# A two-layer trunk on one Trainium2 core: three of the four pairs of output tiles of the FFN's down projection by Strassen's product

## The chip, the core and the metric

The kernel runs on one core of one Trainium2 chip. The metric is the device time in microseconds (us) of one execution, as the median of several runs. TensorE multiplies (PE, its weight loads PEld), VectorE is DVE, ScalarE ACT, GpSimd POOL; SyncE (SP) issues most DMAs.

## The reference

Two layers on x of 512 rows (S) by 1024 columns (D), all in float32; D_FF is 2816.

```python
def conv_ffn(h, up, dw, dw_b, down):
    u = causal_dwconv(h @ up, dw, dw_b)
    gate, val = split_cols(u, [D_FF, D_FF])
    return (jax.nn.silu(gate) * val) @ down
...
# each layer: x = x + mixers(rmsnorm(x)) @ out;  x = x + conv_ffn(rmsnorm(x), ...);  at the end rmsnorm(x)
```

The four mixers (two kinds of attention, RWKV-7, a convolution module) are not touched by the change.

## The kernel before, in words

Everything is held transposed: channels lie on the 128 partitions, the 512 rows of the sequence along the free axis. So x is 8 tiles of 128 x 512 (`x[0..7]`, named x604 to x611 in layer 0's second half), and the FFN's inner activations are 22 tiles.

A float32 product is made of three float16 products. A weight tile is loaded from DRAM in float32 into a staging tile `st` (SP, L196) of 128 x 1024 (8 blocks of 128 x 128) or less, then split into a high part (ScalarE, L211) and a low part (VectorE, L212) in a tile `hl`. Activations are split in the same way. `mm3` (L231 to L236) gives three matmuls for each block of weights, hi x hi, hi x lo and lo x hi; each is 512 columns (the sequence) or 256 wide and loads its own weights.

`weights` (L1118 to L1141) lists all weight tiles of the program in the order of use. `next_w` pops a split tile and keeps `depth` further ones split ahead; `_split` and `w_load` are where the staging tiles come from: two of `wst`, five split tiles of `whl`, and for part of the FFN's tiles a further ring of FST = 2 staging and FHL = 4 split tiles in the FFN's own pool `fp`. Loads and splits are put ahead of other work by a high priority; the order on each engine's queue is fixed when the program is built. An engine works through its queue in that order, and a load waits until its buffer is free.

The up projection is `ffn_up` (L1092 to L1116): 44 tiles of 8 blocks, 24 matmuls each. For each pair (gate, value) the PSUM tile g goes through the three-tap convolution (L1103 ScalarE, L1104 and L1105 VectorE) into u, then tanh, two multiplications (L1109, L1111) and the split into one `act` tile of 2 x 512 (L1113 ScalarE, L1114 VectorE).

The down projection is `project` (L1065 to L1090). For each of 8 output tiles it takes three weight tiles (8, 8 and 6 blocks) and makes 22 x 3 matmuls into one PSUM bank; the last output tile is made in two halves of 256 columns, so that the norm behind it can begin on the first half. `back` (L1027 to L1029) adds a finished product to the residual x on VectorE; `norm_add` (L379 to L390) squares it on ScalarE and adds the squares on GpSimd; `norm_rb` sums over partitions by a matmul on TensorE, and `norm_apply` writes the next layer's input, or `finish` the output. `out_second` (L1044) is the mixers' output projection ahead of the up projection, with the same additions on GpSimd.

```python
        for m in range(NK - tail):
            hls = [self.next_w() for _ in range(nw)]
            ps = self.gbank()
            tile_(ps, hls, full)
            self.back(m, ps, full, scale)
            self.norm_add(m, full, norm_eng)
```

## Time and profile before

| | |
|---|---|
| median of 3 runs | 1348.14 us (1345.51 to 1348.59) |
| profiled execution | 1351.01 us, span 1349.2 us, mean granted clock 0.989 |
| TensorE busy | 1301.4 us (96% of the span) |
| VectorE, ScalarE, GpSimd busy | 903.1, 609.9, 117.7 us |
| DMA | 119.96 MB, 89 GB/s on the mean |

The profile is of one execution on the chip. Busy times are by engine and may overlap; the clock is TensorE's granted share of full speed. In the rows further below a line such as L212 is a line of the kernel; `hl<-st,hl` says what a group of instructions writes and reads.

### The profile page before, as it was taken

To read this page: it belongs to the slowest core of one execution; us is meant where nothing else is said; L and a number is where in the kernel's file an instruction comes from. 1 tells how busy PE (TensorE), PEld (TensorE's weight loads), DVE (VectorE), ACT (ScalarE), POOL (GpSimd) and SP (SyncE) were. 2 spreads that over 40 slices of the span, in tenths; PEclk is the share of its full clock that TensorE was granted. 3 is DMA by queue.
4 is the path that set the end of the run, shared out by engine and by line. 5 is a ranking of instruction groups with operands and counts; after the bars stand their busy time and mean duration, and the time that the engine had idled before them with its cause. 6 is when DMAs were issued, how large, how long until landed. Compare 5 with 4: busy or idle time off the path is not lost.

```text
span 1349.2 us, 22863 instructions
## 1 busy us (share of the span) xinstructions
PE 1301.4 (96%) x9198; PEld 738.1 (55%) x9198; DVE 903.1 (67%) x1770; ACT 609.9 (45%) x1115; POOL 117.7 (9%) x180
## 2 busy tenths in 40 slices
...
GB/s 221 157 85 60 118 33 10 1 71 110 78 94 110 94 109 95 141 167 121 52 101 107 80 78 103 10 3 32 94 51 109 107 96 108 96 103 188 70 28 63
DMA packets 41864, 119.96 MB, mean 89 GB/s; under 512 B 4896, under 2 KB 11680, under 8 KB 41760
## 3 DMA queue, kind: packets, MB, share of 16 engines
...
## 4 chain that ended last, share of the span: by engine, by line
PE 81%; DVE 12%; ACT 2%; DMA 2%; issue 2%; SPq 0%; DVEq 0%; ACTq 0%
PE g L234 21%; PE g L235 21%; PE g L236 21%; DVE cacc L755 4%; PE v L922 3%; PE t L911 2%; DVE hl L212 2%; PE s L891 2%; PE r L578 1%; PE r L234 1%; PE r L235 1%; PE r L236 1%; DVE e L894 1%; DMA st<-in_wi_dram 1%; ACT e L898 1%
## 5 line engine op out<-in xcount | busy, mean ns | idle before, releaser
L236 PE MATMUL g<-hx,hl 128*128 128x512 f16 (+1 forms) x1008 | 368.6, 367 | 0.0
L234 PE MATMUL g<-hx,hl 128*128 128x512 f16 (+1 forms) x1008 | 367.8, 367 | 0.8 <-DVE q L787 0.8
L235 PE MATMUL g<-hx,hl 128*128 128x512 f16 (+1 forms) x1008 | 368.2, 367 | 0.3 <-DVE hx L423 0.3
L212 DVE SCALAR_TENSOR_TENSOR hl<-st,hl 128x1024 f16<-128x1024 f32 (+2 forms) x200 | 238.6, 1195 | 115.8 <-ACT hl L211 114.2
L211 ACT ACTIVATE hl<-st 128x1024 f16<-128x1024 f32 (+2 forms) x200 | 204.4, 1026 | 213.4 <-PE g L236 149.3
L234 PEld LDWEIGHTS <-hl 128*128 128x128 f16 x1724 | 170.1, 99 | 159.5 <-issue 5.2
L236 PEld LDWEIGHTS <-hl 128*128 128x128 f16 x1724 | 169.3, 98 | 157.0 <-issue 2.2
L235 PEld LDWEIGHTS <-hl 128*128 128x128 f16 x1724 | 169.6, 98 | 154.2 <-issue 2.5
L235 PE MATMUL g<-act,hl 128*128 128x512 f16 (+1 forms) x396 | 140.7, 355 | 0.0
L236 PE MATMUL g<-act,hl 128*128 128x512 f16 (+1 forms) x396 | 140.7, 355 | 0.0
L234 PE MATMUL g<-act,hl 128*128 128x512 f16 (+1 forms) x396 | 140.7, 355 | 0.0
L1104 DVE SCALAR_TENSOR_TENSOR u<-g,d_fdw,u 128x511 f32<-128x511 f32 x82 | 61.5, 750 | 95.7 <-ACT u L1103 95.7
L1103 ACT ACTIVATE u<-g,par,d_fdw 128x512 f32<-128x512 f32 x82 | 63.7, 777 | 101.6 <-PE g L236 101.4
L755 DVE SCALAR_TENSOR_TENSOR cacc<-gl,d_cdw,cacc 128x511 f32<-128x511 f32 (+14 forms) x120 | 90.0, 750 | 1.3
L1028 DVE SCALAR_TENSOR_TENSOR x<-g,x 128x512 f32<-128x512 f32 (+1 forms) x62 | 34.9, 568 | 83.3 <-PE g L236 83.1
L909 POOL TENSOR_SCALAR e<-e,den 128x512 f32<-128x512 f32 (+3 forms) x96 | 55.9, 595 | 316.4 <-DVE den L901 207.4
L390 POOL TENSOR_TENSOR acc<-acc,sq 128x256 f32<-128x256 f32 (+1 forms) x38 | 41.7, 1098 | 462.4 <-ACT sq L383 405.5
L894 DVE CUSTOM_DVE_ANT_0 e<-s,con 128x512 f32<-128x512 f32 (+3 forms) x96 | 46.8, 488 | 34.2 <-PE s L891 24.4
L1113 ACT CAST act<-u 128x512 f16<-128x512 f32 x44 | 27.1, 617 | 93.2 <-DVE u L1111 93.2
L1105 DVE SCALAR_TENSOR_TENSOR u<-g,d_fdw,u 128x510 f32<-128x510 f32 x82 | 61.4, 748 | 2.8
L898 ACT ACTIVATE e<-e,mx 128x512 f32<-128x512 f32 (+3 forms) x96 | 53.1, 556 | 17.0 <-DVE mx L896 16.9
L383 ACT ACTIVATE sq<-x 128x256 f32<-128x256 f32 (+1 forms) x54 | 24.5, 467 | 74.9 <-DVE x L1028 71.1
...
## 6 DMA issues: line engine op xcount, KB each, us to landing
st<-in_up_dram SPq DMA_DIRECT2D x88, 512.0 KB, 3.5
st<-in_wi_dram SPq DMA_DIRECT2D x40, 512.0 KB, 3.4
st<-in_dn_dram SPq DMA_DIRECT2D x32, 512.0 KB, 3.7
st<-in_wo_dram SPq DMA_DIRECT2D x16, 512.0 KB, 3.5
st<-in_dn_dram SPq DMA_DIRECT2D x16, 384.0 KB, 3.2
...
```

The costliest lines, as they stand in the source:

```text
L211: act = nc.scalar.activation(hl[:, 0, :cols], st[:, :cols], AF.Copy, scale=SW)
L212: dve = nc.vector.scalar_tensor_tensor(hl[:, 1, :cols], st[:, :cols], SW, hl[:, 0, :cols], op0=ALU.mult, op1=ALU.subtract)
L234: nc.tensor.matmul(ps, hl[:, 0, w], hx[:, 0, cols], start=start, stop=False)
L235: nc.tensor.matmul(ps, hl[:, 0, w], hx[:, 1, cols], start=False, stop=False)
L236: nc.tensor.matmul(ps, hl[:, 1, w], hx[:, 0, cols], start=False, stop=stop)
L755: nc.vector.scalar_tensor_tensor(acc[:, s:512], gl[:, 0:512 - s], wj, acc[:, s:512], op0=ALU.mult, op1=ALU.add)
L894: nc.vector.tensor_tensor_reduce(es[i], ps[:, o:o + w], mask[:, 384 - 128 * t:512], op0=ALU.add, op1=ALU.max, scale=1.0, scalar=-3e38, acc ...
L898: nc.scalar.activation(es[i], es[i], AF.Exp, scale=SC, bias=mx[:, i:i + 1], accum_out=den[:, i:i + 1])
L909: nc.gpsimd.tensor_scalar(es[i], es[i], den[:, i:i + 1], 1.0, op0=ALU.mult, op1=ALU.mult)
L1103: act = nc.scalar.activation(u, ps, AF.Identity, scale=w[:, 88 + ch:89 + ch], bias=self.p("fb", ch))
L1104: stt(u[:, 1:512], ps[:, 0:511], w[:, 44 + ch:45 + ch], u[:, 1:512], op0=ALU.mult, op1=ALU.add)
L1105: dve = stt(u[:, 2:512], ps[:, 0:510], w[:, ch:ch + 1], u[:, 2:512], op0=ALU.mult, op1=ALU.add)
```

## The change

The residual product is y = W^T a, with 8 output tiles and 22 tiles to sum over. The change takes the output tiles in pairs, the channel tiles of the activations in pairs, and the sequence in two halves of 256: each is a 2 x 2 product of blocks, A the weights (A11 to A22), Q the activations (Q11 to Q22). For three of the four pairs of output tiles, `project_fast` makes seven products of blocks (Winograd's form of Strassen's) in place of eight:

- P1 = A11 Q11, P2 = A12 Q21, P4 = A22 T4 use weights as they are; P5 = S1 T1, P6 = S2 T2, P7 = S3 T3 and P3 = S4 Q22 use sums of weights: S1 = A21 + A22, S3 = A11 - A21, S2 = S1 - A11, S4 = A12 - S2. T1 to T4 are differences of activations.
- Each product is 11 blocks x 3 matmuls of 256 columns. `back` adds the finished PSUM tile to the one or two places of x that it belongs to, some after more products have been added to it in PSUM.
- `act_pair` makes T1 to T4 on VectorE, with four subtractions of 256 columns for each pair of channel tiles, and splits two times 1024 columns (Q's, then T's) instead of two times 512.
- `make_sums` loads the four quarters of a pair of output tiles again, in float32, and makes S1 to S4 in place. The first pair is cut into three parts of 4, 4 and 3 blocks; parts 0 and 1 are summed on GpSimd during the up projection, in tiles `dq` that share the buffers of hx; part 2 and the other pairs (two parts of 6 and 5 blocks) on VectorE, in a pool `dp` of ten tiles `dw`, which is opened when the up projection's pool `up` has been closed and takes its place. S tiles are then split as staged weights are.
- The fourth pair is made as before (66 matmuls of 512 columns for tile 6, two halves for tile 7).
- The further ring of staging and split tiles is gone; some split tiles lie in `act` or `dw` buffers.

```diff
-FST, FHL = 2, 4
+DW = 10
...
-        if ring:
-            st = self.fp.tile([128, 1024], F32, tag="fst", bufs=FST, name=self.n("st"))
+
+
+    def w_load(self, src, cols, home=None):
+        if home == "act":
+            st = self.fp.tile([128, 1024], F32, tag="act", bufs=NF // 2, name=self.n("st"))
         else:
             st = self.wst.tile([128, 1024], F32, tag="st", name=self.n("st"))
-        nc.sync.dma_start(st[:, :cols], src)
+        self.nc.sync.dma_start(st[:, :cols], src)
         return st
+
+    def w_pair(self, home):
+        if home == "act":
+            return self.fp.tile([128, 2, 1024], F16, tag="act", bufs=NF // 2, name=self.n("hl"))
+        if home == "dw":
+            return self.dp.tile([128, 2, 768], F16, tag="dw", bufs=DW, name=self.n("hl"))
+        return self.whl.tile([128, 2, 1024], F16, tag="hl", name=self.n("hl"))
...
+        st = src() if callable(src) else self.w_load(src, cols, home)
+        hl = self.w_pair(home)
...
-            self.spare = self.ffn
             return self.stash.pop(0)
         hl = self.next_w()
-
-        ps = self.rbank() if self.spare else self.gbank()
-        self.spare = False
+        ps = self.gbank()
+        for k in range(NK):
+            self.mm3(ps, hl, k, hx[k], slice(0, 512), k == 0, k == NK - 1)
+        return ps
+
+    def gemm_up(self, hx, m):
+
+        if self.stash:
+            if self.todo and len(self.ready) <= self.depth:
+                self.prefetch()
+            return self.stash.pop(0)
+        hl = self.next_w()
+        ps = self.rbank() if m == HEAD else self.gbank()
...
-    def project(self, rhs, order, tail, scale, norm_eng):
-        nc = self.nc
-        nk = len(order)
...
+    Q12, Q11, Q22, Q21, T3, T1, T2, T4 = range(8)
+
+    def act_pair(self, fp, q):
+
+        nc = self.nc
+        a = fp.tile([128, 2, 8 * 256], F16, tag="act", bufs=NF // 2, name=self.n("act"))
+        src = q.rearrange("p a b -> p (a b)")
+
+        def split(cols):
+            nc.scalar.copy(a[:, 0, cols], src)
+            nc.vector.tensor_tensor(a[:, 1, cols], src, a[:, 0, cols], op=ALU.subtract)
+
+        def sub(o, i, j):
+            nc.vector.tensor_tensor(q[:, o % 4], q[:, i % 4], q[:, j % 4], op=ALU.subtract)
+
+        split(slice(0, 1024))
+        sub(self.T1, self.Q12, self.Q11)
+        sub(self.T3, self.Q22, self.Q12)
+        sub(self.T2, self.Q22, self.T1)
+        sub(self.T4, self.Q21, self.T2)
+        split(slice(1024, 2048))
+        return a
+
+
+    FAST = {"P1": ("A11", Q11), "P2": ("A12", Q21), "P3": ("S4", Q22), "P4": ("A22", T4), "P5": ("S1", T1),
+            "P6": ("S2", T2), "P7": ("S3", T3)}
+    RAW = {"A11": (0, 0), "A12": (0, 1), "A21": (1, 0), "A22": (1, 1)}
+
+
+    PARTS = (((0, 4), (4, 8), (8, 11)),) + (((0, 6), (6, 11)),) * 3
+
+    def fast_order(self, mp):
+        n = range(len(self.PARTS[mp]))
+        if mp:
+            return [(p, h) for p in ("P1", "P5", "P6", "P3", "P7", "P2", "P4") for h in n]
+        raw = ("P1", "P2", "P4")
+        return ([(p, h) for p in raw for h in n[:-1]] + [(p, n[-1]) for p in raw] +
+                [(p, h) for p in ("P5", "P6", "P3", "P7") for h in n])
...
+    def down_items(self, l):
+        items = []
+        for mp in range(NK // 2 - 1):
+            for p, h in self.fast_order(mp):
+                w = self.FAST[p][0]
+                src, n = self.quarter(l, mp, w if w in self.RAW else "A11", h)
+                if w not in self.RAW:
+                    src = lambda w=w, key=(mp, h): self.sums[key][w]
+                items.append((src, n))
+        for w in ("A11", "A12", "A21", "A22"):
+            for h in range(2):
+                items.append(self.quarter(l, NK // 2 - 1, w, h) + (("dw",) if w[1] == "2" else ()))
+        return items
+    def make_sums(self, l, mp, h):
+        nc = self.nc
+        b = {}
+        for name in ("A22", "A11", "A21", "A12"):
+            src, n = self.quarter(l, mp, name, h)
+            if mp == 0 and h < 2:
+                t = self.hxp.tile([128, 512], F32, tag="hx", bufs=NK, name=self.n("dq"))
+            else:
+                t = self.dp.tile([128, 768], F32, tag="dw", bufs=DW, name=self.n("dw"))
+            b[name] = t[:, :n]
+            nc.sync.dma_start(b[name], src)
+        tt = (nc.gpsimd if mp == 0 and h < 2 else nc.vector).tensor_tensor
+        tt(b["A22"], b["A21"], b["A22"], op=ALU.add)
+        tt(b["A21"], b["A11"], b["A21"], op=ALU.subtract)
+        tt(b["A11"], b["A22"], b["A11"], op=ALU.subtract)
+        tt(b["A12"], b["A12"], b["A11"], op=ALU.subtract)
+        self.sums[mp, h] = {"S1": b["A22"], "S2": b["A11"], "S3": b["A21"], "S4": b["A12"]}
+    def project_fast(self, l, acts, scale, norm_eng):
+        c1, c2 = self.HALVES[1], self.HALVES[0]
+        full = slice(0, 512)
+        self.make_sums(l, 0, 2)
+        self.after = ()
+        ahead = {0: {9: 0, 15: 1}, 1: {5: 0, 9: 1}, 2: {}}
+        for mp in range(NK // 2 - 1):
+            m = 2 * mp
+            parts, order = self.PARTS[mp], self.fast_order(mp)
+            x = {"11": (m, c1), "12": (m, c2), "21": (m + 1, c1), "22": (m + 1, c2)}
+            A, B, C = self.gbank()[:, 0:256], self.rbank()[:, 0:256], self.rbank()[:, 0:256]
+            reg = {"P1": A, "P2": B, "P3": C, "P4": A if mp else self.rbank()[:, 0:256], "P5": C, "P6": A, "P7": A}
+            adds = {"P1": ("11",), "P2": ("11",), "P5": ("22",), "P6": ("12",), "P3": ("12",),
+                    "P7": ("22",) if mp else ("22", "21"), "P4": ("21",)}
+            seen = set()
+            for step, (p, h) in enumerate(order):
+                if step in ahead[mp]:
+                    self.make_sums(l, mp + 1, ahead[mp][step])
+                r = reg[p]
+                q = 256 * self.FAST[p][1]
+                k0, k1 = parts[h]
+                hl = self.next_w()
+                for k in range(k0, k1):
+                    self.mm3(r, hl, k - k0, acts[k], slice(q, q + 256), k == k0 and id(r) not in seen,
+                             k == k1 - 1, True)
+                seen.add(id(r))
+                if h < len(parts) - 1:
+                    continue
+                for o in adds[p]:
+                    self.back(x[o][0], r, x[o][1], scale)
+            for i in range(2):
+                self.norm_add(m + i, full, norm_eng)
...
+        m = NK - 2
+        ps = self.gbank()
+        tile_(ps, [self.next_w() for _ in range(4)], full)
+        self.back(m, ps, full, scale)
+        self.norm_add(m, full, norm_eng)
         self.depth = HEAD
-        hls = [[self.next_w() for _ in range(nw)] for _ in range(tail)]
+        m += 1
+        hls = [self.next_w() for _ in range(4)]
         for cols in self.HALVES:
-            for i in range(tail):
-                m = NK - tail + i
-                ps = self.gbank()[:, 0:256]
-                tile_(ps, hls[i], cols)
-                self.back(m, ps, cols, scale)
-                self.norm_add(m, cols, nc.vector if m < NK - 1 else None)
+            ps = self.gbank()[:, 0:256]
+            tile_(ps, hls, cols)
+            self.back(m, ps, cols, scale)
+            self.norm_add(m, cols)
             yield cols
...
+            if i in (NF - 8, NF - 5):
+                self.make_sums(l, 0, int(i == NF - 5))
+            if i == NF - 2:
+                self.depth = 4
...
-            nc.vector.tensor_tensor(us[0], us[0], us[1], op=ALU.mult)
-            a = fp.tile([128, 2, 512], F16, tag="act", bufs=NF, name=self.n("act"))
-            nc.scalar.copy(a[:, 0], us[0])
-            nc.vector.tensor_tensor(a[:, 1], us[0], a[:, 0], op=ALU.subtract)
-            acts.append(a)
+            if i % 2 == 0:
+                q = up.tile([128, 4, 256], F32, tag="q", bufs=1, name=self.n("q"))
+            nc.vector.tensor_tensor(q[:, 2 * (i % 2):2 * (i % 2) + 2].rearrange("p a b -> p (a b)"), us[0], us[1],
+                                    op=ALU.mult)
+            if i % 2:
+                acts.append(self.act_pair(fp, q))
...
-                items.append((a["up"][l, m], 1024, m < HEAD or m % 2 == 1))
-            for m in range(NK):
-                for g in range(3):
-                    k1 = min(8, NF - 8 * g) * 128
-                    items.append((a["dn"][l, m, :, 1024 * g:1024 * g + k1], k1, m == NK - 1 or (3 * m + g) % 2 == 1))
+                items.append((a["up"][l, m], 1024, "act" if m < HEAD else None))
+            items += self.down_items(l)
...
+                with pool(f"up{l}") as up:
+                    hf = self.new_hx(up, "hf")
+                    for cols in self.out_second(OTAIL):
+                        self.norm_apply(self.d["gf"], hf, cols)
+                    self.gemm_head(hf, HEAD)
+                    self.depth = 2
+                    acts = self.ffn_up(l, fp, up, hf)
...
-                for cols in self.project(acts, range(NF), 1, 1.0 / (SW * SA), nc.gpsimd):
+                with pool(f"dp{l}") as self.dp:
+                    for cols in self.project_fast(l, acts, 1.0 / (SW * SA), nc.gpsimd):
```

The list of weights in DRAM is laid out for this by quarters. In the order rows that follow, hl is a split weight tile, st a staged one, dq and dw quarters of weights or their sums, q a pair's Q's or T's, act its split tile, x the residual, g and r PSUM banks.

VectorE of the changed kernel, layer 0, from the last splits of activations (L1089) to the first sum (L1152) of the down projection:

```order
L215 SCALAR_TENSOR_TENSOR hl997_5948<-st996_5946,hl997_5948 128x384
L1092 TENSOR_TENSOR q944_5734<-q944_5734 128x256
L215 SCALAR_TENSOR_TENSOR hl998_5963<-dq863_5167,hl998_5963 128x512
L1092 TENSOR_TENSOR q944_5734<-q944_5734 128x256
L215 SCALAR_TENSOR_TENSOR hl999_5978<-dq897_5406,hl999_5978 128x512
L1039 SCALAR_TENSOR_TENSOR x604_3375<-g984_5874,x604_3375 128x256
L1092 TENSOR_TENSOR q944_5734<-q944_5734 128x256
L1039 SCALAR_TENSOR_TENSOR x604_3375<-r985_5875,x604_3375 128x256
L1089 TENSOR_TENSOR act954_5808<-q944_5734,act954_5808 128x1024
L1039 SCALAR_TENSOR_TENSOR x605_3376<-r987_5877,x605_3376 128x256
L1152 TENSOR_TENSOR dw980_5862<-dw982_5866,dw980_5862 128x384
```

All of these are new: the last split of the T's stands behind the split of the last raw weights of the first pair and two splits of sums, and the first sum on VectorE behind it.

SP of the changed kernel at the same place, the loads of the first pair's last raw parts, of the second pair's first raw tiles, and of the quarters for the sums (L1150):

```order
L196 DMA st992_5912<-in_dn_dram 128x384
L196 DMA st994_5929<-in_dn_dram 128x384
L196 DMA st996_5946<-in_dn_dram 128x384
L196 DMA st1018_6157<-in_dn_dram 128x768
L196 DMA st1020_6172<-in_dn_dram 128x640
L1150 DMA dw980_5862<-in_dn_dram 128x384
L1150 DMA dw981_5864<-in_dn_dram 128x384
L1150 DMA dw982_5866<-in_dn_dram 128x384
L1150 DMA dw983_5868<-in_dn_dram 128x384
L1150 DMA dw1002_6017<-in_dn_dram 128x768
```

Before, this queue held staged weights alone; now the quarters stand in it, and dw981 lies where tiles of the up projection were.

VectorE at the end of layer 0's down projection, before:

```order
L1028 SCALAR_TENSOR_TENSOR x609_3380<-g1013_6220,x609_3380 128x512
L212 SCALAR_TENSOR_TENSOR hl1024_6379<-st1023_6377,hl1024_6379 128x768
L212 SCALAR_TENSOR_TENSOR hl1032_6399<-st1031_6397,hl1032_6399 128x1024
L1028 SCALAR_TENSOR_TENSOR x610_3381<-g1021_6306,x610_3381 128x512
L1028 SCALAR_TENSOR_TENSOR x611_3382<-g1033_6402,x611_3382 128x256
```

and of the changed kernel:

```order
L215 SCALAR_TENSOR_TENSOR hl1091_6865<-st1090_6863,hl1091_6865 128x768
L215 SCALAR_TENSOR_TENSOR hl1093_6870<-st1092_6868,hl1093_6870 128x640
L215 SCALAR_TENSOR_TENSOR hl1096_6945<-st1095_6943,hl1096_6945 128x1024
L215 SCALAR_TENSOR_TENSOR hl1098_6950<-st1097_6948,hl1098_6950 128x1024
L1039 SCALAR_TENSOR_TENSOR x610_3381<-g1085_6852,x610_3381 128x512
L215 SCALAR_TENSOR_TENSOR hl1100_6955<-st1099_6953,hl1100_6955 128x1024
L215 SCALAR_TENSOR_TENSOR hl1102_6960<-st1101_6958,hl1102_6960 128x1024
L1039 SCALAR_TENSOR_TENSOR x611_3382<-g1103_6963,x611_3382 128x256
```

The update of x610 (output tile 6) now has four splits right ahead of it, the last two of the next layer's first weights (hl1096, hl1098).

## Rows read from the trace of the kernel before

**Rows 1.** The page: busy us (share of span) and instructions by engine; chain by engine.
```profile
PE 1301.4 (96%) x9198; PEld 738.1 (55%) x9198; DVE 903.1 (67%) x1770; ACT 609.9 (45%) x1115; POOL 117.7 (9%) x180
...
PE 81%; DVE 12%; ACT 2%; DMA 2%; issue 2%; SPq 0%; DVEq 0%; ACTq 0%
```
**Rows 2.** Windows of layer 0's up and down projection: PE, PEld, DVE, ACT, POOL, clock, DMA, GB/s.
```profile
331.00:560.00 229.00, 228.98 (x1166) 113.72 (x1164) 164.81 (x234) 106.16 (x146) 1.07 (x2) 1.00 0.30 94
560.00:675.00 115.00, 115.00 (x601) 58.62 (x600) 38.86 (x48) 30.77 (x36) 10.71 (x7) 1.00 0.39 124
```
**Rows 3.** Timeline of PE (start, us, instruction), first and last of each stretch.
```profile
554.80 0.38 PE L236 MATMUL g<-hx,hl 128*128 128x512 f16 x1
...
560.41 0.38 PE L235 MATMUL g<-hx,hl 128*128 128x512 f16 x1
...
663.83 0.27 PE L234 MATMUL g<-act,hl 128*128 128x256 f16 x1
...
667.65 0.27 PE L236 MATMUL g<-act,hl 128*128 128x256 f16 x1
```
**Rows 4.** Groups of PEld by form: xcount | busy us, mean ns | idle before, releaser.
```profile
L235 PEld LDWEIGHTS <-hl 128*128 128x128 f16 x1724 | 169.6, 98 | 154.2 <-issue 2.5
```
**Rows 5.** Groups of DVE by form, the same columns.
```profile
L212 DVE SCALAR_TENSOR_TENSOR hl<-st,hl 128x1024 f16<-128x1024 f32 x176 | 215.8, 1227 | 88.9 <-ACT hl L211 87.3 <-PE g L236 1.2
...
L1114 DVE TENSOR_TENSOR act<-u,act 128x512 f16<-128x512 f32 x44 | 30.4, 691 | 26.0 <-ACT act L1113 26.0
...
L423 DVE TENSOR_TENSOR hx<-nt,hx 128x256 f16<-128x256 f32 x64 | 26.1, 426 | 0.5
...
L212 DVE SCALAR_TENSOR_TENSOR hl<-st,hl 128x768 f16<-128x768 f32 x16 | 15.3, 955 | 26.8 <-ACT hl L211 26.8
...
L1028 DVE SCALAR_TENSOR_TENSOR x<-g,x 128x256 f32<-128x256 f32 x28 | 11.6, 420 | 26.8 <-PE g L236 26.6
```
**Rows 6.** Groups of ACT by form: the splits of 1024 and 768 columns.
```profile
L211 ACT ACTIVATE hl<-st 128x1024 f16<-128x1024 f32 x176 | 184.5, 1050 | 155.9 <-PE g L236 98.8 <-DMA st<-in_wi_dram 19.9 <-DMA st<-in_dn_dram 14.6
...
L211 ACT ACTIVATE hl<-st 128x768 f16<-128x768 f32 x16 | 13.4, 840 | 37.3 <-PE g L236 32.5 <-issue 4.6 <-DMA st<-in_dn_dram 0.2
```
**Rows 7.** Groups of POOL by form: the norm's additions of 512 columns.
```profile
L390 POOL TENSOR_TENSOR acc<-acc,sq 128x512 f32<-128x512 f32 x14 | 21.7, 1547 | 441.9 <-ACT sq L383 385.2 <-issue 56.6
```
**Rows 8.** Timeline of SP: start, us that one issue takes, load.
```profile
606.17 0.33 SPq L196 DMA_DIRECT2D st<-in_wi_dram  x1
```
**Rows 9.** DMA issues of the whole span: xcount, KB each, median us to landing.
```profile
st<-in_wi_dram SPq DMA_DIRECT2D x40, 512.0 KB, 3.4
...
st<-in_dn_dram SPq DMA_DIRECT2D x16, 384.0 KB, 3.2
...
con<-in_con_dram SPq DMA_DIRECT2D x1, 64.0 KB, 2.9
...
pos<-in_pos_dram ACTq DMA_DIRECT2D x2, 8.0 KB, 2.5
```
**Rows 10.** Timeline of DVE: an instruction that starts before the last has ended.
```profile
443.50 0.75 DVE L1105 SCALAR_TENSOR_TENSOR u<-g,d_fdw,u 128x510 f32<-128x510 f32 x1
444.17 1.21 DVE L212 SCALAR_TENSOR_TENSOR hl<-st,hl 128x1024 f16<-128x1024 f32 x1
```
**Rows 11.** Tile st on SP from 560 to 605 us: its 15 loads' landings.
```profile
DMA to landing us min/median/max: 3.1/4.2/5.0
```
**Rows 12.** Windows at two other places, columns as in rows 2.
```profile
175.00:178.40 3.40, 1.47 (x10) 0.74 (x12) 3.40 (x8) 2.40 (x7) 0.00 (x0) 1.00 0.15 24
178.40:181.90 3.50, 3.50 (x46) 3.26 (x46) 3.18 (x8) 0.62 (x2) 1.41 (x2) 0.51 0.34 126
...
717.70:721.10 3.40, 1.85 (x38) 1.19 (x30) 2.97 (x14) 0.80 (x5) 0.00 (x0) 1.00 0.44 131
721.10:728.00 6.90, 6.24 (x16) 2.42 (x17) 5.47 (x9) 2.61 (x7) 0.00 (x0) 0.51 0.11 45
```
**Rows 13.** Window of dense loads at the start of layer 1's mixers.
```profile
692.70:696.30 3.60, 3.60 (x35) 3.22 (x34) 1.66 (x2) 1.74 (x3) 0.00 (x0) 1.00 0.88 281
```

More of the change, by code (lines that the diff above doesn't have):

```diff
@@ L163, in __init__ @@
         self.after = ()
-        self.ffn = self.spare = False
+        self.ffn = False
     def n(self, s="t"):
@@ L201, in w_split, with _split @@
             return self._split(*item)
-    def _split(self, src, cols, ring=False):
+    def _split(self, src, cols, home=None):
         nc = self.nc
-        st = self.w_load(src, cols, ring)
-        if ring:
-            hl = self.fp.tile([128, 2, 1024], F16, tag="fhl", bufs=FHL, name=self.n("hl"))
-        else:
-            hl = self.whl.tile([128, 2, 1024], F16, tag="hl", name=self.n("hl"))
-        act = nc.scalar.activation(hl[:, 0, :cols], st[:, :cols], AF.Copy, scale=SW)
-        dve = nc.vector.scalar_tensor_tensor(hl[:, 1, :cols], st[:, :cols], SW, hl[:, 0, :cols],
-                                             op0=ALU.mult, op1=ALU.subtract)
-        for later, earlier in zip((act, dve), self.after):
+        st = src() if callable(src) else self.w_load(src, cols, home)
+        hl = self.w_pair(home)
+        hi = nc.scalar.activation(hl[:, 0, :cols], st[:, :cols], AF.Copy, scale=SW)
+        lo = nc.vector.scalar_tensor_tensor(hl[:, 1, :cols], st[:, :cols], SW, hl[:, 0, :cols],
+                                            op0=ALU.mult, op1=ALU.subtract)
+        for later, earlier in zip((hi, lo), self.after):
             self.order(later, earlier)
@@ new lines, in quarter @@
+    def quarter(self, l, mp, name, h):
+        k0, k1 = self.PARTS[mp][h]
+        i, j = self.RAW[name]
+        return self.a["dn"][l, 2 * mp + i, j, :, 128 * k0:128 * k1], 128 * (k1 - k0)
+    def down_items(self, l):
[11 more added lines that the diff above has]
+        return items
@@ new lines, in project_fast @@
+    def project_fast(self, l, acts, scale, norm_eng):
[30 more added lines that the diff above has]
+                self.norm_add(m + i, full, norm_eng)
+        def tile_(ps, hls, cols):
+            n = 0
+            for (odd, h), hl in zip(((0, 0), (0, 1), (1, 0), (1, 1)), hls):
+                k0, k1 = self.PARTS[-1][h]
+                for k in range(k0, k1):
+                    self.mm3(ps, hl, k - k0, acts[k],
+                             slice(512 * odd + cols.start, 512 * odd + cols.stop), n == 0, n == NF - 1)
+                    n += 1
+        m = NK - 2
[3 more added lines that the diff above has]
+        self.norm_add(m, full, norm_eng)
@@ L1090, in project, with ffn_up @@
             yield cols
[L1092 removed]
+    def ffn_up(self, l, fp, up, hx):
         nc = self.nc
```

53 lines of the change are left out of this document (18 added, 35 removed).

## The prediction, made before the changed kernel was run

> **What bounds the kernel now.** I read the page's busy times and its chain first. TensorE is busy 96% of the span and holds 81% of the chain that ended last [rows 1]: time falls only where TensorE gets less to do, or rises where it is made to wait. Then the windows of layer 0's up and down projections [rows 2]: PE is busy 228.98 of 229.00 us and 115.00 of 115.00, while VectorE has 64.2 us and 76.1 us to spare. So today every split, load and norm of the FFN is hidden, and one matmul saved is one step saved. All this is against the profiled execution, 1351.0 us (span 1349.2 and 1.8 around it); the median of the runs shown, 1348.1, lies 2.9 lower, and I shift the result by that.
>
> **1. Matmuls, on the path.** The timeline of PE [rows 3] has 27 matmuls of 512 columns from start to start in 5.61 us, 26 steps of 0.2158 us, and 36 of 256 columns in 3.82 us, 35 steps of 0.1091. The first three pairs lose 6 tiles x 66 = 396 wide steps per layer, 85.5 us, and get 3 x 7 x 33 = 693 narrow ones, 75.6 us. Saved: 9.85 per layer, **-19.7**. That narrow step is also near its weight load: one takes 98 ns on average [rows 4], and in [rows 3] each narrow matmul has a new one. The two timelines give no sign of a toll for narrowness beyond 1.2 ns. The Trainium skill (TensorEngine Tiling (Array Packing), Instruction Overhead) puts some 60 cycles on each matmul; at 2.4 GHz that is 25 ns, and by it the gain would be 6.2 instead of 19.7 us and the sum 13.5 worse. The 35 measured steps disagree with that rule, so I keep 19.7; rival D has the remainder.
>
> **2. Up projection, hidden.** A pair of channel tiles loses two subtractions of 0.691 on VectorE, and gets two of 1024 columns, 1.22 by the split's row, and four of 0.43 [rows 5]: +2.8 us a pair, 30.6 a layer out of 64.2 free. ScalarE splits twice the columns in as many casts, 1.05 at most each [rows 6]: under 12 us, with 106.16 busy of 229 [rows 2]. GpSimd gets eight sums of 1.55 [rows 7], 12.4 us, with 1.07 us of work there now [rows 2]. The cover is TensorE's 229 us of up tiles; were the 30.6 bare, they would eat the whole gain. One exception: GpSimd's first four sums, 6.2 us, stand ahead of the norm's additions in the output projection. GpSimd mostly idles for squares there [rows 7], so only loads that land late make this felt. I take +0.3 per layer, 0 to 2: **+0.6**. The up weights now queued on SP behind the sums' eight loads, 0.33 us each to issue [rows 8], are needed over 20 us later: nothing.
>
> **3. Start of the down projection, a new wait.** The order of VectorE shows that act954, the last split of activations, stands behind hl997; and on SP the load dw981, first operand of the first pair's third sum, overlays tiles of the up pool that this split still reads. Behind dw981 on SP stand all loads of the next sums; on TensorE everything stands behind S1's third part. The chain from the last up matmul, with L one landing: that matmul's end and a 512-column split 1.52 (0.2 + 0.63 + 0.69); L of a staged load; hi and lo of 384 columns 1.08; L; 1.08; VectorE's five subtractions and splits in order plus one update 2.6; cast and subtraction of 1024 columns 2.27 [rows 5, 6]; issue 0.33; L; addition 0.55 and hi split 0.53. That is 9.96 + 3L. Meanwhile TensorE has raw products for some 121 narrow steps, 13.2 us. L of 192 KB is not in the trace: 64 KB took 2.9, 384 KB 3.2, the ends are 2.5 (8 KB) and 3.4 (512 KB) [rows 9]. I take 3.05, between the nearest two: 19.1 - 13.2 = 5.9 idle per layer, **+11.8**; 8.5 with 2.5, 13.9 with 3.4. No shorter way exists in the order: nothing else may pass these waits. The Trainium skill (DMA: Bandwidth & Descriptors, Anatomy of one DMA) fits 2.0 us plus bytes over 436 GB/s, 2.45 for this load; by it the sum would be 3.6 lower. For 384 KB that fit gives 2.9, where the row has 3.2, so it is low here.
>
> **4. VectorE behind it.** From S1's third part on, VectorE owes the rest of pair one's splits (6.3), three more sums (1.7), five updates (2.1), the second pair's eight sums (7.1) and its first three splits (2.7): 19.9, less 0.08 for each of some 33 starts ahead of the instruction before [rows 10], 17.2 us. TensorE reaches the second part of the second pair's S1 after 159 steps, 17.3 us. Nothing is to spare, and each sum waits for four fresh loads: where SP's loads stand dense, landings are 3.1, 4.2, 5.0 (least, median, most) [rows 11], 1.15 over my L at the median. I take that once per layer, **+2.4** (0 to 8). Later pairs have each product's 3.6 us of TensorE against 1.8 of splits, 0.4 to 0.8 of updates and at most 2.4 of sums, without a burst: nothing.
>
> **5. End of layer 0's down projection.** The ring is gone, two staging buffers are left, and the update of x610 now stands behind hl1096 and hl1098, next layer's weights, on VectorE. From the third pair's P6 on, these come in rounds: the first split 2.05; five rounds of issue, landing and two 768-column splits, 5.17 each; the 512 KB load 3.73; 1.05, 1.23 and 1.15; update 0.69, square 0.62 (both by columns), GpSimd addition 1.55 [rows 5 to 9]: 37.9, with 0.6 between engines 38.5. TensorE has 132 narrow steps 14.4, 66 wide 14.2, 66 narrow 7.2: 35.8. The norm's matmul so waits 2.7, **+2.7** (0 to 6; 0 if a round is 0.55 shorter). The last layer has no next weights: nothing.
>
> **6. The clock.** In two places of the trace where TensorE was busy only part of a stretch, 1.47 of 3.40 us and 1.85 of 3.40, the granted clock was 0.51, 1.2 GHz, in the next 3.5 and 6.9 us, and 1.00 (2.4 GHz) before [rows 12]. Waits 3 (twice) and 5 are as long as these. A lowering with dense work behind costs half its length: 1.7 us by the first row, 3.4 by the second if all of it were dense. I take 1.7 three times: **+5.1** (0 to 10.2).
>
> **Sum:** -19.7 + 0.6 + 11.8 + 2.4 + 2.7 + 5.1 = **+2.9 us**, 1353.9 for an execution like the profiled one, 1348.1 + 2.9 = **1351.0** for a median. A measurement of this kernel can tell about 0.3%, 4.0 us, from no change: by the sum it is no change.
>
> **The rivals.**
> **A, the sum** (1351.0; 1345 to 1357 by its inner bounds), 0.47: the saved matmuls are given back, mainly at one wait.
> **B, slower: the second pair's sums starve.** Place: VectorE's S1 of pair two, whose eight loads (2.9 MB) can only be issued from dw981 on. They must land within some 9 us, 319 GB/s. For it: in a dense stretch of 3.60 us at a DMA share of 0.88 the kernel moved 281 GB/s [rows 13]. Against: that stretch is of other loads and had no deadline. From about 250 GB/s on, the last load is 2.5 us late; TensorE then idles 2.5 more per layer, with a further lowering of 1.7: 2 x 4.2 = +8.4, 1359.4. Chance 0.25.
> **C, faster: short landings, quick clock.** If 192 KB lands in 2.5 us, wait 3 is 4.25 per layer (8.5) and wait 5 nil (its rounds give back 2.75); with a lowering for waits 3 alone (3.4) and no lateness in 4: -19.7 + 0.6 + 8.5 + 3.4 = -7.2, 1340.9. For it: the 8 KB row; against it: all rows of weights. The landing that the Trainium skill's fit gives lies at this end. Chance 0.25.
> **D, the change doesn't give what it says:** narrow steps under a constant change of weights are dearer than 0.1091. At 0.1233 the 1386 of them eat the whole gain: 1370.7. Only [rows 4], 98 ns against 109, speaks for it, the 36 steps of [rows 3] against. It is where that skill's 60 cycles would lead (131.7 ns a step). Chance 0.03.
>
> **How the numbers follow.** Likeliest is A, so 1351.0 us. The range goes to C's 1341 below and past B's 1359 above, 1340 to 1361; outside lie D, half of C's lower part and B's doubled form (some 0.2). Within 0.3% is 1344.1 to 1352.2: A gives 0.33 of its 0.47, and C's upper part 0.05: 0.38. Faster: C 0.20 and A 0.02, 0.22. Slower: B 0.25, D 0.03, A 0.12: 0.40.
>
> **What would show it.** In the profile after: PE with 1386 steps of 0.109 us in 256 columns on act tiles; at each layer's last up tile a PE gap of about 6 us (in two or three pieces) released by a split of S1's third part, SP's load dw just before it; granted clock near 0.5 right behind; VectorE near 85% in the up projection without a PE gap; at layer 0's end a norm matmul waiting for GpSimd. Wrong would be: no gap at the start of the down projection (the chain of 3), gaps inside the up projection (2), or gaps from pair to pair that recur (4, B).

## The result, and the profile after

The changed kernel takes 1358.76 us (median of 4 runs, 1357.59 to 1361.14) against 1348.08 before, run beside it: ratio 1.0085, interval 1.0067 to 1.0104. It is slower, by more than the 0.3% that can be told. The prediction said 1351.0 and "no change"; the time lies in its range (1340 to 1361), on the side to which it gave 0.40, and close to rival B's 1359.4, but not by B's mechanism.

The page after, busy times and the chain, answers to [rows 1]:

```profile
PE 1290.7 (95%) x9792; PEld 798.5 (59%) x9792; DVE 1034.7 (76%) x1996; ACT 659.0 (48%) x1181; POOL 140.0 (10%) x196
...
PE 67%; DVE 18%; DMA 7%; ACT 4%; issue 3%; POOL 1%; SPq 0%; DVEq 0%; ACTq 0%; POOLq 0%
```

PE is busy 10.7 us less, and the span (1359.3) is 10.1 longer: PE is idle 20.8 us more. The saved matmuls are worth 19.7, so by an estimate from these two numbers some 9 us of PE's busy time are matmuls that ran longer, at a lower clock. PE's share of the chain fell from 81% to 67%; VectorE and DMA have it now. PE's waits, grouped by who waited for whom (total us, times, longest):

```profile
PE t L418 <- DVE y L298: 12.4, 4, 5.9
PE r L238 <- ACT hl L214: 7.6, 2, 3.9
...
PE g L238 <- DVE x L1039: 5.5, 5, 2.0
...
PE s L414 <- POOL acc L401: 4.2, 1, 4.2
```

The second is the start of the down projection, the fourth is layer 0's end; both were forecast. The other two were not. The two longest of the third lie in the output projection. The first is the norms' wait for a square root; its two new waits (1.2 and 1.4) lie in the norm ahead of the up projection. Before the change it was:

```profile
PE t L407 <- DVE y L287: 9.7, 2, 5.8
```

To see where the time went I cut each profile at five places of PE's timeline: the first wide matmul of the output projection's second pass, the start of its last matmul, the first wide matmul of the up projection, the end of its last, and the end of the down projection. In the change, layer 0, the last four are these rows:

```profile
334.68 0.27 PE L240 MATMUL g<-y,hl 128*128 128x256 f16 x1
...
358.35 0.38 PE L238 MATMUL r<-hx,hl 128*128 128x512 f16 x1
...
565.55 0.38 PE L240 MATMUL g<-hx,hl 128*128 128x512 f16 x1
...
685.56 0.27 PE L240 MATMUL g<-act,hl 128*128 128x256 f16 x1
```

The four stretches between these places, for all kernels (us, layer 0 / layer 1; e1 to e8 are the experiments below):

| | output projection, 2nd pass | to the first wide up tile | up | down |
|---|---|---|---|---|
| before | 24.77 / 24.77 | 22.32 / 22.31 | 207.36 / 207.37 | 114.85 / 114.85 |
| change | 27.62 / 27.70 | 23.67 / 23.90 | 207.58 / 207.58 | 119.90 / 112.21 |
| e1 | 24.93 / 24.92 | 22.32 / 22.32 | 207.58 / 207.58 | 117.68 / 112.05 |
| e2 | 27.57 / 27.67 | 23.72 / 23.64 | 207.59 / 207.58 | 116.75 / 110.15 |
| e3 | 27.81 / 27.44 | 23.64 / 23.64 | 207.58 / 207.59 | 112.03 / 112.42 |
| e4 | 24.93 / 24.93 | 22.32 / 22.32 | 207.58 / 207.58 | 109.81 / 109.55 |
| e5 | 24.93 / 24.92 | 22.32 / 22.32 | 207.58 / 207.58 | 109.03 / 109.07 |
| e6 | 26.10 / 25.58 | 26.92 / 28.42 | 207.58 / 207.58 | 118.91 / 112.09 |
| e7 | 24.93 / 24.93 | 22.32 / 22.32 | 207.58 / 207.58 | 110.34 / 109.30 |
| e8 | 24.93 / 24.93 | 22.32 / 22.31 | 207.36 / 207.37 | 108.79 / 108.59 |

The change against before: +5.8 and +2.9 in the first two columns, +0.4, and +2.4 in the last, 11.5. All the rest of the span, mixers above all, is 1.4 shorter in this profile, which no run here explains (its code is the same).

**The output projection and the norm.** Row by row, in layer 0 of the change, ACT's timeline, then POOL's, then one row each of VectorE's and PE's:

```profile
316.38 1.06 ACT L214 ACTIVATE hl<-st 128x1024 f16<-128x1024 f32 x1 [2.53 <-DMA st<-in_up_dram]
...
322.50 0.42 ACT L394 ACTIVATE sq<-x 128x256 f32<-128x256 f32 x1 [2.58 <-POOL acc L401]
```

```profile
314.09 1.26 POOL L1152 TENSOR_TENSOR dq<-dq,dq 128x512 f32<-128x512 f32 x1 [4.44 <-DMA dq<-in_dn_dram]
...
318.13 2.13 POOL L1155 TENSOR_TENSOR dq<-dq,dq 128x512 f32<-128x512 f32 x1
320.22 3.85 POOL L401 TENSOR_TENSOR acc<-acc,sq 128x512 f32<-128x512 f32 x3
...
340.33 1.33 POOL L1153 TENSOR_TENSOR dq<-dq,dq 128x512 f32<-128x512 f32 x1
341.74 1.40 POOL L1154 TENSOR_TENSOR dq<-dq,dq 128x512 f32<-128x512 f32 x1
```

```profile
317.47 1.66 DVE L215 SCALAR_TENSOR_TENSOR hl<-st,hl 128x1024 f16<-128x1024 f32 x1 [1.75 <-ACT hl L214]
```

```profile
319.52 0.27 PE L238 MATMUL g<-y,hl 128*128 128x256 f16 x1 [1.90 <-DVE x L1039]
```

ScalarE's half of a split waits 2.53 us for an up weight that now lands behind the quarters, and VectorE's half takes 1.66 us beside a sum of GpSimd, 1.21 to 1.27 in this stretch without one. A square waits 2.58 for GpSimd, which does sums until 320.26. Both hold up the updates of x, and PE waits (1.90 before its matmul at 319.52). The second four sums run while VectorE takes the norm's square root, in steps of 2 columns. VectorE there:

```profile
339.48 1.05 DVE L434 TENSOR_TENSOR hx<-nt,hx 128x256 f16<-128x256 f32 x1
340.46 1.23 DVE L288 TENSOR_SCALAR ti<-u 128x2 int32<-128x2 int32 x1
341.60 0.41 DVE L434 TENSOR_TENSOR hx<-nt,hx 128x256 f16<-128x256 f32 x1
341.94 1.23 DVE L289 TENSOR_SCALAR y<-ti 128x2 int32<-128x2 int32 x1
```

L288 and L289 have 2 columns and take 1.23 us each; they end at 341.69 and 343.17, near the ends of the GpSimd sums at 341.66 and 343.14. The norm's matmul behind them waits 1.16 us.

**The down projection's start.** SP, DVE, ACT and PE, each from its own timeline (a fence for each):

```profile
574.86 0.42 SPq L1150 DMA_DIRECT2D dw<-in_dn_dram  x1
...
579.36 4.74 SPq L1150 DMA_DIRECT2D dw<-in_dn_dram  x9
```

```profile
578.10 1.23 DVE L1089 TENSOR_TENSOR act<-q,act 128x1024 f16<-128x1024 f32 x1 [0.78 <-ACT act L1088]
...
582.39 0.56 DVE L1152 TENSOR_TENSOR dw<-dw,dw 128x384 f32<-128x384 f32 x1 [2.16 <-DMA dw<-in_dn_dram]
```

```profile
583.06 0.52 ACT L214 ACTIVATE hl<-dw 128x384 f16<-128x384 f32 x1 [4.99 <-DVE dw L1152]
```

```profile
579.38 0.27 PE L239 MATMUL r<-act,hl 128*128 128x256 f16 x1 [0.46 <-DVE act L1089]
...
583.64 0.40 PE L238 MATMUL r<-act,hl 128*128 128x256 f16 x1 [3.88 <-ACT hl L214]
```

The landings of the first two loads behind the split, dw981 and dw982, from the view of tile dw from 579.3 to 579.75 us, and those of the staged loads of the same size, from the list of DMA issues:

```profile
L1150 SPq DMA_DIRECT2D dw<-in_dn_dram x2: 328/380/432, 579.4 to 579.7; - x2
...
DMA to landing us min/median/max: 2.4/2.5/2.6
```

```profile
st<-in_dn_dram SPq DMA_DIRECT2D x6, 192.0 KB, 2.3
```

That is the forecast chain, link by link: dw981 goes at 579.36, when the last split has ended (579.33). S1 is not made of dw981 but of dw980 and dw982; dw982 stands behind dw981 on SP, goes at 579.73 and lands 2.57 us later. The sum starts at 582.39, and S1's third part lets PE go at 583.64. The windows of this wait and behind it, those of the wait at layer 0's end (4.19 us, for GpSimd's addition), and the one behind the start's wait in layer 1, columns as in [rows 2]:

```profile
578.90:583.64 4.74, 0.40 (x3) 0.10 (x2) 1.99 (x5) 0.58 (x2) 0.00 (x0) 0.79 0.55 145
583.64:587.00 3.36, 3.36 (x16) 2.18 (x17) 3.36 (x7) 2.65 (x5) 0.00 (x0) 0.50 1.02 383
587.00:590.50 3.50, 3.50 (x27) 2.86 (x26) 2.51 (x5) 1.14 (x3) 0.00 (x0) 0.79 1.00 389
...
670.70:674.90 4.20, 0.04 (x1) 0.04 (x1) 2.35 (x3) 1.69 (x3) 1.27 (x1) 0.87 0.68 210
674.90:678.00 3.10, 3.10 (x15) 2.45 (x16) 1.73 (x2) 1.06 (x1) 0.00 (x0) 0.50 0.61 186
678.00:681.00 3.00, 3.00 (x19) 2.19 (x16) 0.82 (x2) 0.42 (x1) 0.00 (x0) 0.57 0.66 212
...
1252.24:1257.40 5.16, 5.16 (x24) 3.43 (x25) 5.16 (x10) 2.98 (x6) 0.00 (x0) 0.50 1.00 361
```

Where PE had been idle the clock is 0.50, half of 2.4 GHz, and then back: 3.36 x 0.50 + 3.50 x 0.21 = 2.4 us lost at the start, 3.10 x 0.50 + 3.00 x 0.43 = 2.8 at the end, 5.16 x 0.50 = 2.6 in layer 1.

Rival B's starving doesn't show here: behind the wait the loads run at 383 and 389 GB/s, where B asked whether 319 could be had, and from there to the norm's matmul at layer 0's end PE has one idle time above 0.2 us, of 0.38.

### The profile page after: what moved, and what is told of

Its sections match the earlier page's. It is cut to its first block, busy times and chain, and to the rows that moved or that the text cites. A ratio compares the mean times of both kernels' runs of the same rounds, so it can differ in the third digit from the quotient of the medians.

```text
span 1359.3 us, 24606 instructions
## 1 busy us (share of the span) xinstructions
PE 1290.7 (95%) x9792; PEld 798.5 (59%) x9792; DVE 1034.7 (76%) x1996; ACT 659.0 (48%) x1181; POOL 140.0 (10%) x196
## 3 DMA queue, kind: packets, MB, share of 16 engines
HBM read 127.28 MB, written 4.19 MB: 97 GB/s over the span
## 4 chain that ended last, share of the span: by engine, by line
PE 67%; DVE 18%; DMA 7%; ACT 4%; issue 3%; POOL 1%; SPq 0%; DVEq 0%; ACTq 0%; POOLq 0%
PE g L238 16%; PE g L240 16%; PE g L239 16%; DVE hl L215 4%; DVE cacc L766 4%; PE v L933 3%; DMA st<-in_dn_dram 2%; DMA st<-in_wi_dram 2%; PE t L922 2%; ACT hl L214 2%; PE r L238 2%; PE r L239 2%; PE r L240 2%; PE s L902 2%; PE r L589 1%
## 5 line engine op out<-in xcount | busy, mean ns | idle before, releaser
L215 DVE SCALAR_TENSOR_TENSOR hl<-st,hl 128x1024 f16<-128x1024 f32 (+5 forms) x210 | 234.0, 1114 | 88.9 <-ACT hl L214 88.5
L214 ACT ACTIVATE hl<-st 128x1024 f16<-128x1024 f32 (+5 forms) x210 | 200.1, 953 | 174.3 <-PE g L240 66.2
L238 PEld LDWEIGHTS <-hl 128*128 128x128 f16 x1922 | 190.8, 99 | 143.4 <-ACT hl L214 8.9
L239 PEld LDWEIGHTS <-hl 128*128 128x128 f16 x1922 | 190.1, 99 | 134.9 <-issue 8.1
L240 PEld LDWEIGHTS <-hl 128*128 128x128 f16 x1922 | 189.9, 99 | 134.5 <-issue 3.4
L238 PE MATMUL g<-act,hl 128*128 128x256 f16 (+1 forms) x374 | 109.0, 292 | 0.4 <-DVE x L1039 0.4
L240 PE MATMUL g<-act,hl 128*128 128x256 f16 (+1 forms) x374 | 109.0, 291 | 0.2 <-DVE hl L215 0.2
L239 PE MATMUL g<-act,hl 128*128 128x256 f16 (+1 forms) x374 | 109.0, 292 | 0.0
L1089 DVE TENSOR_TENSOR act<-q,act 128x1024 f16<-128x1024 f32 x44 | 53.7, 1221 | 20.6 <-ACT act L1088 20.6
L1088 ACT CAST act<-q 128x1024 f16<-128x1024 f32 x44 | 45.7, 1039 | 46.4 <-DVE q L1242 42.2
L238 PE MATMUL r<-act,hl 128*128 128x256 f16 x220 | 60.8, 276 | 7.6 <-ACT hl L214 7.6
L1039 DVE SCALAR_TENSOR_TENSOR x<-g,x 128x256 f32<-128x256 f32 (+1 forms) x74 | 36.3, 497 | 34.2 <-PE g L240 33.8
```

What stands on the lines that cost most here:

```text
L214: hi = nc.scalar.activation(hl[:, 0, :cols], st[:, :cols], AF.Copy, scale=SW)
L215: lo = nc.vector.scalar_tensor_tensor(hl[:, 1, :cols], st[:, :cols], SW, hl[:, 0, :cols], op0=ALU.mult, op1=ALU.subtract)
L238: nc.tensor.matmul(ps, hl[:, 0, w], hx[:, 0, cols], start=start, stop=False, **kw)
L239: nc.tensor.matmul(ps, hl[:, 0, w], hx[:, 1, cols], start=False, stop=False, **kw)
L240: nc.tensor.matmul(ps, hl[:, 1, w], hx[:, 0, cols], start=False, stop=stop, **kw)
L1089: nc.vector.tensor_tensor(a[:, 1, cols], src, a[:, 0, cols], op=ALU.subtract)
```

## The experiments

**e1: the sums' loads in their place among the up weights.**

```diff
-        self.nc.sync.dma_start(st[:, :cols], src)
+        self.last_dma = self.nc.sync.dma_start(st[:, :cols], src)
...
-            nc.sync.dma_start(b[name], src)
+            dma = nc.sync.dma_start(b[name], src)
+            if mp == 0 and h < 2:
+                self.order(dma, self.last_dma)
```

> Edit: the loads of the quarters for the first pair's sums (parts 0 and 1) may not be issued ahead of the up weights near which the program asks for them, so SP keeps the up weights first, and GpSimd's eight sums fall into the middle of the up projection. Theory N (sums collide with the output projection and its norm): in the profile of the change the stretch from the output projection's second pass to the second half of the norm is 40.8 and 41.1 us in the two layers, where it was 36.6; it goes back to 36.6, so 8.7 us less, about 1350.1. Rival R (the ring of staging and split buffers is missed there, so the up projection's first weights are late whatever the sums do): the stretch stays at 40 or more, 1357 to 1359. Under N VectorE's instructions of 2 columns in the second norm, some of which take 1.1 to 1.2 us, go back to 0.17; under R they too stay.

Measured: 1349.28 us, ratio to before 1.0011 (0.9999 to 1.0023). Pass and norm are back at 24.93 and 22.32 in both layers, and VectorE's steps at 0.16:

```profile
335.82 0.16 DVE L288 TENSOR_SCALAR ti<-u 128x2 int32<-128x2 int32 x1
...
336.31 0.16 DVE L289 TENSOR_SCALAR y<-ti 128x2 int32<-128x2 int32 x1
```

N holds, R falls: with the ring missing the pass is 0.16 us longer than before, and the sums cost nothing in the middle of the up projection (207.58 as in the change).

**e2: other places for the tiles of the up pool**, by a first tile of each kind ahead of the inputs `hf`.

```diff
+                    for tag, shape, bufs in (("u", [128, 512], 4), ("fth", [128, 512], 2), ("q", [128, 4, 256], 1)):
+                        up.tile(shape, F32, tag=tag, bufs=bufs, name=self.n("first"))
                     hf = self.new_hx(up, "hf")
```

> Edit: the order in which the tiles of the up projection's pool get their places is turned round, so that the quarters of the first pair's third sum overlay the inputs of the up projection (free with its last matmul) and tiles u, and no longer the tile q that the last split reads. Theory W (the load behind that split is what the start of the down projection waits for): the gap of 3.9 and 3.7 us ahead of S1's third part shrinks to under 1.5 us in each layer, and the 4.5 us at half clock behind it go: 4 to 6 us per layer, 1347 to 1351. Rival V (VectorE and the burst of loads are the limit, and the wait only moves to the next sums): the gap falls, but later waits of the down projection grow by as much, and the time stays within 3 us of 1358.8.

Measured: 1353.8 us, ratio 1.0027 (1.0012 to 1.0042). The longer wait fell from 3.9 and 3.7 us to 1.6 and 2.5, and the down projection by 3.2 and 2.1: W is right about the load, too high by half. dw982 now goes before the last split, but it lands in 4.2 us instead of 2.6, at 579.73, and the sum, which on VectorE also stands behind the last split and an update, starts at 579.87. And the clock still falls in layer 0, to 0.52 for the next 3.4 us:

```profile
581.20:584.60 3.40, 3.30 (x17) 2.12 (x18) 3.40 (x7) 2.57 (x5) 0.00 (x0) 0.52 0.98 333
```

**e3: the update ahead of the next layer's splits.**

```diff
...
-        self.back(m, ps, full, scale)
-        self.norm_add(m, full, norm_eng)
+        dve = self.back(m, ps, full, scale)
+        self.after = self.norm_add(m, full, norm_eng), dve
```

`self.after` holds the instructions behind which the next split on ScalarE and on VectorE is put.

> Edit: the splits of the next layer's first weights are put behind the update of output tile 6 and its square, on VectorE and ScalarE. Theory U (the update stands behind the splits of late weights): the norm's matmul no longer waits 4.2 us for GpSimd at layer 0's end, and the clock isn't lowered there; from layer 0's second half of the norm to the end of its down projection 338.0 us become about 330.5, 1351.5. Rival L (the loads are late in any case, and the next layer's first matmuls wait for the same weights instead): the wait moves behind the norm, and the time is 1356 or more.

Measured: 1353.43 us, ratio 1.0033 (1.002 to 1.0045). Layer 0's down projection takes 112.03 instead of 119.90 us, as layer 1's, and PE has no idle time at that layer's end: U. VectorE has the update of output tile 6 behind two splits of 1024 columns in the change, and ahead of them in e3:

```profile
670.85 1.23 DVE L215 SCALAR_TENSOR_TENSOR hl<-st,hl 128x1024 f16<-128x1024 f32 x1 [1.32 <-ACT hl L214]
671.99 0.68 DVE L1039 SCALAR_TENSOR_TENSOR x<-g,x 128x512 f32<-128x512 f32 x1
```

```profile
663.22 0.69 DVE L1040 SCALAR_TENSOR_TENSOR x<-g,x 128x512 f32<-128x512 f32 x1
666.32 1.23 DVE L215 SCALAR_TENSOR_TENSOR hl<-st,hl 128x1024 f16<-128x1024 f32 x1 [2.41 <-ACT hl L214]
```

**e4: all three.**

> All three edits. If N, W and U hold and don't overlap: 1358.8 - 8.7 - 10 - 7.3 = 1333, that is 15 us under the kernel before (1348.1), ratio about 0.989. If the rivals hold for one of them: 1340 to 1343. If they hold for all: 1355 or more.

Measured: 1338.56 us, ratio 0.9924 (0.9908 to 0.9941): faster than before. The single edits add up but for 3 us (ratios against the change's 1.0085: 0.74, 0.58 and 0.52%, in sum 1.84%, measured 1.61%). The time lies 5.6 us above the 1333 that I gave if all three theories held in full, and under the 1340 to 1343 for one rival: by their medians the single edits brought 9.5, 5.0 and 5.3 us, where I had put down 8.7, 10 and 7.3.

**e5: more cover for the first pair's third part**, on e4.

```diff
-                [(p, h) for p in ("P5", "P6", "P3", "P7") for h in n])
+                [(p, h) for p in ("P5", "P6") for h in n[:-1]] + [(p, n[-1]) for p in ("P5", "P6")] +
+                [(p, h) for p in ("P3", "P7") for h in n])
```

> Edit: the three of e4, and in the first pair the first two parts of P6 (24 narrow matmuls, 2.6 us, with sums that GpSimd has made) are set ahead of the third part of P5. In e4 two pieces of wait are left at the start of each down projection (0.5 and 1.6 us), with the clock at 0.64 and 0.86 in the 7 us behind them; there the third sum on VectorE stands behind the update of P4, which stands behind the last split. Theory K (a wait of this size costs its own length and about as much again by the clock): with the longer wait covered, both go, about 3.5 us per layer, 1338.6 - 7 = 1331.5. Rival V (VectorE is the limit there: P6's splits now stand ahead of the sum and push it back by as much as they cover): the wait stays at 1 us or more and the time within 2 us of 1338.6.

Measured: 1337.54 us, ratio 0.9916 (0.9898 to 0.9933); the down projection 109.03 and 109.07. The wait is 1.3 us in one piece and the clock no longer falls, yet only 0.5 to 0.8 us per layer are won, and the intervals of e4 and e5 overlap. V's numbers come true, but not its reason. VectorE stands idle for 1.69 us just ahead of the sum, for a product of TensorE whose update is queued before it, and dw982 had landed at 573.86, 1.5 us before the sum starts: the place in the queue holds the sum back.

```profile
575.06 0.42 DVE L1040 SCALAR_TENSOR_TENSOR x<-r,x 128x256 f32<-128x256 f32 x1 [1.69 <-PE r L240]
```

Behind the sum VectorE is busy 3.45 of 3.60 us, then 4.00 of 4.00, while the clock stays at 1.00:

```profile
575.40:579.00 3.60, 1.86 (x13) 0.94 (x13) 3.45 (x8) 1.76 (x4) 0.00 (x0) 1.00 0.92 316
579.00:583.00 4.00, 4.00 (x38) 3.38 (x37) 4.00 (x8) 2.77 (x6) 0.00 (x0) 1.00 0.89 308
```

Much of what the clock gave back goes into later waits for VectorE, in layer 0 these at the second pair, a small form of what B feared, which e4 does not have:

```profile
597.12 0.27 PE L238 MATMUL r<-act,hl 128*128 128x256 f16 x1 [0.65 <-DVE x L1040]
...
597.85 0.28 PE L240 MATMUL g<-act,hl 128*128 128x256 f16 x1 [0.36 <-DVE hl L215]
```

**e6: GpSimd's additions alone later**, on the change.

```diff
...
-        tt(b["A22"], b["A21"], b["A22"], op=ALU.add)
+        first = tt(b["A22"], b["A21"], b["A22"], op=ALU.add)
+        if mp == 0 and h < 2:
+            self.order(first, self.last_add)
```

`self.last_add` is the norm's last addition on GpSimd so far.

> Edit, on the changed kernel: the loads of the first pair's quarters keep their early places on SP, ahead of the up weights, but GpSimd's eight sums stand behind all its additions for the norm. It parts the two ways in which e1 can have worked. Theory P (GpSimd: its sums hold up the squares and the norm): the second pass of the output projection, 27.6 us in the change and 24.9 in e1, goes back to 24.9 or near it. Theory S (SP: the up weights behind the sums' loads land late, and their splits on VectorE hold up the updates): it stays at 27 or more. For the second half of the norm, where all eight sums now run beside VectorE's steps of 2 columns: if GpSimd holds VectorE up there, the stretch from the end of the pass to the first full up tile, 23.7 in the change and 22.3 in e1, stays above 23.3 or grows. Time 1350 to 1356 under P, 1357 to 1360 under S.

Measured: 1361.84 us, ratio 1.0089 (1.0067 to 1.0111). The pass fell from 27.6 and 27.7 to 26.1 and 25.6: of the 2.7 and 2.8 us above e1, GpSimd's sums in the pass hold 1.5 and 2.1; the rest, 1.2 and 0.7, I put down to the loads on SP, by difference; neither P nor S alone. The time I gave for P was wrong, because all eight sums now run beside the norm, and that stretch grew to 26.92 and 28.42, 4.6 and 6.1 above 22.3. VectorE there:

```profile
333.51 1.15 DVE L434 TENSOR_TENSOR hx<-nt,hx 128x256 f16<-128x256 f32 x1
334.58 0.47 DVE L432 SCALAR_TENSOR_TENSOR nt<-x,d_gf,t 128x256 f32<-128x256 f32 x1
334.97 1.10 DVE L434 TENSOR_TENSOR hx<-nt,hx 128x256 f16<-128x256 f32 x1
```

Beside a GpSimd sum the subtraction L434, with both operands in SBUF, takes 1.02 to 1.48 in most places, and 0.41 without; L432, which has one operand in PSUM, stays at 0.47.

**e7: the second and third pair without the arithmetic of their sums**, on e4.

> Edit, on e4: the additions and subtractions of the second and third pair are left out (the quarters are loaded and split as they are), so VectorE has 8 x 0.955 + 8 x 0.82 = 14.2 us less per layer; the output is that of other weights. Rival B of the prediction (the second pair's sums are the limit behind the start): the down projection, 109.8 and 109.5 us in e4, falls by 2 us or more per layer. If it falls by less than 0.5, VectorE's sums of these pairs and their catch-up cost nothing on the path, and what is left above 105.0 us is the first pair's wait and the clock.

Measured (one run): 1340.01 us; the down projection 110.34 and 109.30, against 109.81 and 109.55 in e4. VectorE with 14.2 us less to do per layer wins nothing here: in e4 these sums do not starve TensorE, and rival B is not what happens.

**e8: the first pair plain**, on e2 and e3.

```diff
-    PARTS = (((0, 4), (4, 8), (8, 11)),) + (((0, 6), (6, 11)),) * 3
+    PARTS = (((0, 6), (6, 11)),) * 4
...
+        for m in range(2):
+            self.make_sums(l, 1, m)
+            ps = self.gbank()
+            tile_(ps, [self.next_w() for _ in range(4)], full)
+            self.back(m, ps, full, scale)
+            self.norm_add(m, full, norm_eng)
...
-        for mp in range(NK // 2 - 1):
+        for mp in range(1, NK // 2 - 1):
```

> Edit: Strassen's product for the second and third pair only; the first pair is made plainly, as the fourth is (two output tiles of 66 wide matmuls, 28.5 us), while the second pair's quarters are loaded and summed on VectorE; no sums on GpSimd; the edits of e2 and e3 stay. One pair's saving, 3.28 us per layer, is given up. Theory K (what is left above 105.0 us in e4 and e5, 4.0 to 4.8 us per layer, is the price of starting with the first pair's split weights, sums and last split at once, not of VectorE as a whole): with 28.5 us of plain work as a cover nothing waits, and the down projection takes 114.85 - 2 x 3.28 = 108.3 us, 1335 to 1337. Rival V (VectorE's sums are too much in any place): the wait moves to the second pair's S1, and the down projection takes 110 us or more, 1339 or later.

Measured: 1334.36 us (1333.69 to 1335.94), ratio 0.9903 (0.9887 to 0.992), the lowest median of all, with one Strassen pair less (e5's interval overlaps it). Theory K holds: the down projection takes 108.79 and 108.59, 0.3 to 0.5 above the 108.3 of the bare count of steps, and in layer 0 PE is busy all through the stretch shown, with the clock at 1.00:

```profile
553.00:660.00 107.00, 107.00 (x758) 73.97 (x756) 70.39 (x90) 41.67 (x55) 9.04 (x7) 1.00 0.52 162
```

## Why the prediction was off, step by step

- **Step 1, right.** From 566.42 to 573.30 us the change has 63 steps of narrow matmuls, 0.1092 each. Rival D is out. By an estimate from the 60 cycles that the Trainium skill (TensorEngine Tiling (Array Packing), Instruction Overhead) puts on each matmul, a step would be 0.13; the trace disagrees, with its 0.1092.
- **Step 2 failed, at the exception and at its last sentence.** "GpSimd mostly idles for squares there [rows 7], so only loads that land late make this felt", +0.6 in all, and "nothing" for the up weights behind the sums' loads. Measured: +5.8 in the pass and +2.9 before the up projection, 8.7 us. The profiles differ by 10.1 us where 2.9 were forecast, so this term alone is larger than the miss. The long idle in [rows 7] is a sum over the whole span; in the pass GpSimd has an addition to make for nearly every tile, and some 6 us of sums ahead of them delay all that comes behind. The up weight behind the loads landed late enough for its split to wait 2.53 us. I also priced a sum by GpSimd's own time alone, and left out the second four sums, which fall beside the norm. While a sum runs, VectorE's instructions stretch: L434 from 0.41 to 1.05, L288 from 0.16 to 1.23. The Trainium skill (GPSIMD Engine Reference, Specifications) says that GpSimd shares its SBUF interfaces with VectorE, with contention for instructions of two SBUF inputs or in a two-port mode. L434 agrees with the first part; which part covers L288 no run here shows. The rest of step 2 held: the up projection's +0.2 is two early matmuls of the down projection, VectorE is 82% busy there (170.23 of 207.40).
- **Step 3, right in mechanism, 1.6 and 1.8 too high:** 4.3 and 4.1 us of wait instead of 5.9. The term that was off is L. The three landings of the chain took 2.43, 2.24 and 2.57 us instead of 3.05 each, 1.9 less in all; the chain took 17.9 us from the last up matmul instead of 19.1, so its other links were 0.7 longer, 0.37 of it dw982's place behind dw981. The nearest rows of other sizes in [rows 9] misled; rival C had the size right, with 2.5 for a landing and a wait of 4.25. The fit that step 3 quotes from the Trainium skill (DMA: Bandwidth & Descriptors, Anatomy of one DMA) gives an estimate of 2.45, and the trace agrees, with 2.24 to 2.57, though the page has the fit for transfers that GpSimd issues, and these are SP's.
- **Step 4, in size half of the forecast:** 2.4 us were put down for both layers (twice 1.15 is 2.3). From the end of up to the fourth pair's first wide matmul the change takes 83.1 and 82.7 us, where 75.6 are narrow steps; less the waits 4.3 and 4.1 and the clock 2.4 and 2.6 this leaves 0.8 and 0.4.
- **Step 5, mechanism right (e3), size 1.5 too low:** 4.19 against 2.7.
- **Step 6, right in sign, too low:** 2.4, 2.6 and 2.8 against 1.7 each, since the clock came back later than I took it. e3 shows that it goes with the wait: without the wait at layer 0's end the clock stays at 1.00 there. How much a wait costs is less certain. In e3's layer 1 a wait of 4.0 us at the start, close to the 4.1 of the change, cost 3.30 x 0.50 = 1.7 us of clock by the windows below, not 2.6, so in the table's last column differences of 1 us between single profiles can be the clock's and not the edit's.

```profile
1244.10:1247.40 3.30, 3.30 (x16) 2.10 (x17) 3.30 (x7) 2.59 (x5) 0.00 (x0) 0.50 0.96 317
1247.45:1250.80 3.35, 3.35 (x33) 3.00 (x32) 2.37 (x5) 1.42 (x4) 0.00 (x0) 1.00 1.01 374
```

That the time lies in the range is in part luck. Steps 2, 5 and 6 were together 12.3 us too low, steps 3 and 4 together 4.6 too high, and the range reached so far up only for rival B, which did not happen. Nor are the saved matmuls given back "mainly at one wait", as A has it: the norm and the pass took 8.7 us, the start's waits 8.4, the clock 7.8, layer 0's end 4.2.
